# A hybrid decoder trunk: the last pair of output tiles of the first MLP as two plain tiles, and the mLSTM's sums of squares and gates three to five steps earlier

## The chip, the cores and the metric

The kernel runs on one core of one Trainium2 chip. The metric is the device time of one execution in microseconds (us), as the median of several runs. Engines are named as in the profile: PE is TensorE's matmul, PEld its weight load, DVE is VectorE, ACT is ScalarE, POOL is GpSimd, SP is SyncE, which issues most transfers. Times inside an execution are microseconds from the start of the profiled span.

## The reference

Two layers on 512 tokens of 1024 features. Layer 0 is a differential attention followed by an MLP; layer 1 is an mLSTM mixer followed by an MLP. Each part is normed on its way in and added back.

```python
for layer in range(DEPTH):                 # 2
    mix = diff_attention(rmsnorm(h, ...)) if layer == 0 else mlstm_mixer(rmsnorm(h, ...))
    h = h + mix
    h = h + sqrelu_mlp(rmsnorm(h, mlp_norm[layer]), mlp_w1[layer], mlp_w2[layer])
return rmsnorm(h, final_norm)

def sqrelu_mlp(h, w1, w2):                 # 1024 -> 4096 -> 1024
    return jnp.square(jax.nn.relu(h @ w1)) @ w2

def mlstm_mixer(h, w_in, b_i, b_f, conv_w, conv_b, head_norm_w, w_out):
    proj = h @ w_in                        # q and k, v, output gate, 2 x 4 gates
    ...
    i_pre = gates[..., :ML_HEADS] + b_i
    log_f = jax.nn.log_sigmoid(gates[..., ML_HEADS:] + b_f)
    ht = mlstm_chunkwise(q, k, v, i_pre, log_f)
```

## The kernel before

**Layout.** The residual `h` stays on the chip, transposed, as eight tiles `h[0]` to `h[7]` of 128 features by 512 tokens; `h2[i]` is the pair `h[2i]`, `h[2i+1]`. Products are made from split operands: a value is a high part in fp32r (made on ACT, line 254 at the bottom of `split` and `operand`) and a low part (the rest, made on DVE, line 528 or 513), and each product is three matmuls: high by high, low by high, high by low. Weights come in units of 512 KB: a DMA from SP into a `raw` tile, then a split into `whi` and `wlo`. There are three `raw`, `whi` and `wlo` tiles in a ring and one more of each (`rawx`, `whix`, `wlox`) inside an MLP.

**Steps.** PE's order is the order of the program. `tick()` counts steps: one step is three matmuls of 512 columns, or six of 264 in the mLSTM's first product. `after(n, f)` runs `f` n steps later, which puts f's matmuls at that place of PE's order. The other engines' instructions are put in order by the framework's scheduler, each engine in order from then on.

**The MLP.** `hidden` makes one hidden tile: ReLU, scaling, square, and sums and differences of blocks of 256 tokens in `chains`, seven blocks of which are split into a slot `uh`, `ul` (line 885). `down(q, i)` adds quarter q of the hidden tiles into the pair of output tiles i. It computes the 2 by 2 block product with seven block products in place of eight (28 steps: 7 products by 4 hidden pairs, by 3 matmuls of 256 columns, lines 922 to 924). For it the two weight units are split in four pieces: `first`, `half`, and two pieces of sums of weights (`sums1` and `sums2`, lines 365 to 370, results in `wsums`). Its results are joined on DVE in `work` (lines 937 to 940) and added to the pair at once (line 945); then each of the two tiles becomes the next part's operand: `x_xh` on ACT, its square on ACT, `x_xl` on DVE (line 513), and the square is added to `acc` on POOL (line 524). The last call is `down(3, 3)`, which makes `h[6]` and `h[7]`. In the second MLP that last pair is made in another way, by `finish`, with the blocks that `spare` keeps (line 887); this is there before and after.

**The mLSTM's start.** `vpair_mm(x, 264)` multiplies the first 256 value columns and the 8 gate columns: for each of the eight operand tiles k in turn, 12 matmuls (lines 432 to 434) into four banks. Then eight `ntile_mm` make the tiles of q and k (lines 400 to 402, 24 matmuls of 512 columns each), one of which goes through `evict_qk` when it is done: a product with the scale `rs` (line 1026), the convolution's three multiply-adds (line 1030), a sigmoid, a split.

- `token_scale` (T_MRS = 22 steps after the start): splits `acc`, sums it over features with two matmuls by `ones_d` (lines 535, 536), and makes the scale `rs` from it (lines 559, 552, 553, 561 on DVE; logarithm, exponential, table load, square on ACT).
- `gates` (T_GATES = 14 steps after the first product): `token_cols` turns `rs` with four transposes (line 569), DVE copies column `rscol` out of them, then come the gates and the eviction of the values (line 582). The third q and k tile takes the first of the value banks.
- `gate_rows` (T_GROWS = 30) transposes the gates (line 1067) and makes running sums on DVE (lines 1068 to 1082); `gate_cols` (T_GCOLS = 60) transposes the rows `ig` back (line 1087).
- `head(hd)` starts 15 steps after the last q and k tile: its `scores` are made of line 1106 (gates), exponentials on ACT, line 1117 and on.

## Time and profile before

| | us |
|---|---|
| median of 3 runs | 1186.81 (1186.56 to 1188.86) |
| the profiled execution | 1188.99 |
| its span in the profile | 1187.3 |
| PE busy | 1144.2 (96% of the span) |
| DVE busy | 915.3 (77%) |
| ACT busy | 608.5 (51%) |
| POOL busy | 184.6 (16%) |
| PE's share of the chain that ended last | 77% |
| DVE's share of it | 14% |

The profile is of one execution. The lines of the page that show busy shares cut the span into 40 slices of 29.7 us, in tenths; PEclk is the clock that was granted to TensorE, in tenths of 2.4 GHz. Matmuls are pipelined, so the distance between the starts of two matmuls, not the duration of one, is what PE needs for it. A number in brackets at the end of a row is the time that the engine sat idle before that instruction, with what released it.

### The profile page before, as it was taken

Reading aid. Unit: us, or ns where it says so; the run is one execution under the profiler, and the core shown is the slowest. Engines: PE = TensorE matmul, PEld = TensorE weight load, DVE = VectorE, ACT = ScalarE, POOL = GpSimd, SP = SyncE. Lnnn points to the kernel's source line nnn. Section 1 sums busy time; section 2 is a strip of 40 time slices with the busy share of each in tenths; the row PEclk is TensorE's granted clock in tenths of the full one; section 3 lists DMA queues with packets and bytes.
Section 4 is the critical chain, followed back from the end, with each engine's and each line's share of the span. In section 5 each row is a group of like instructions: output and inputs, shape, how many; then the busy total and the mean of one; then the engine's idle time right before and its main releaser. Section 6 shows DMA issues by size and latency. Waiting matters only on the chain.

```text
span 1187.3 us, 17224 instructions
## 1 busy us (share of the span) xinstructions
PE 1144.2 (96%) x6730; PEld 1006.3 (85%) x6730; DVE 915.3 (77%) x1384; ACT 608.5 (51%) x917; POOL 184.6 (16%) x178
## 2 busy tenths in 40 slices
PE   7799999999999999999988899999999999999996
PEld 5688888888998998998977778887889889889895
DVE  7679888577976967966979957667598688687786
ACT  5477777564534434534545457574454354353453
POOL 5432332040000000000221212224000000000001
PEclk9899999999999999999999999999999999999998
DMA  6622222243164273371231221223425524625412
GB/s 204 187 66 79 81 71 79 65 130 118 54 177 133 70 188 108 90 192 57 73 113 39 89 71 52 74 71 91 135 77 137 148 90 126 172 70 145 145 36 71
DMA packets 36593, 123.92 MB, mean 104 GB/s; under 512 B 4351, under 2 KB 6418, under 8 KB 36512
## 3 DMA queue, kind: packets, MB, share of 16 engines
q1 hardware_dynamic: 30288, 103.38, 27.6%
q0 software_dynamic: 5104, 17.87, 7.7%
q10 hardware_dynamic: 1120, 1.57, 0.4%
q8 instruction: 53, 0.87, 0.3%
q14 instruction: 28, 0.23, 0.1%
HBM read 108.11 MB, written 4.74 MB: 95 GB/s over the span
## 4 chain that ended last, share of the span: by engine, by line
PE 77%; DVE 14%; ACT 4%; issue 2%; DMA 2%; POOL 0%; DVEq 0%; SPq 0%; ACTq 0%; POOLq 0%
PE bank L401 15%; PE bank L402 15%; PE bank L400 15%; PE bank L923 8%; PE bank L924 8%; PE bank L922 8%; DVE wlo L528 2%; DVE tmp_tmp L1030 1%; PE bank L434 1%; PE bank L433 1%; PE bank L432 1%; DMA raw<-wgt 1%; DVE x_xl L513 1%; ACT whi L254 1%; PE bank L730 1%
## 5 line engine op out<-in xcount | busy, mean ns | idle before, releaser
L400 PE MATMUL bank<-x_xh,whi 128*128 128x512 f32 x640 | 253.5, 396 | 4.8 <-DVE vl_v L582 2.5
L402 PE MATMUL bank<-x_xh,wlo 128*128 128x512 f32 x640 | 255.0, 398 | 1.0 <-DVE wlo L528 1.0
L401 PE MATMUL bank<-x_xl,whi 128*128 128x512 f32 x640 | 254.4, 398 | 0.6 <-DVE x_xl L513 0.6
L254 ACT ACTIVATE whi<-raw 128x1024 fp32r<-128x1024 f32 (+2 forms) x128 | 133.4, 1043 | 124.5 <-PE bank L923 47.8
L528 DVE TENSOR_TENSOR wlo<-raw,whi 128x1024 fp32r<-128x1024 f32 (+2 forms) x128 | 160.6, 1255 | 34.3 <-ACT whi L254 33.7
L923 PE MATMUL bank<-ul,whi 128*128 128x256 f32 x560 | 157.8, 282 | 0.1
L922 PE MATMUL bank<-uh,whi 128*128 128x256 f32 x560 | 157.9, 282 | 0.0
L924 PE MATMUL bank<-uh,wlo 128*128 128x256 f32 x560 | 157.8, 282 | 0.0
L400 PEld LDWEIGHTS bank<-x_xh,whi 128*128 128x128 f32 x640 | 122.5, 191 | 32.9 <-DVE vl_v L582 3.0
L402 PEld LDWEIGHTS bank<-x_xh,wlo 128*128 128x128 f32 x640 | 120.9, 189 | 28.7 <-DVE wlo L528 1.9
L401 PEld LDWEIGHTS bank<-x_xl,whi 128*128 128x128 f32 x640 | 121.1, 189 | 27.9 <-DVE x_xl L513 1.3
L923 PEld LDWEIGHTS bank<-ul,whi 128*128 128x128 f32 x560 | 105.7, 189 | 0.5 <-DVE ul L528 0.3
L922 PEld LDWEIGHTS bank<-uh,whi 128*128 128x128 f32 x560 | 106.0, 189 | 0.1
L924 PEld LDWEIGHTS bank<-uh,wlo 128*128 128x128 f32 x560 | 105.8, 189 | 0.0
L943 POOL DMA_DIRECT2D h<-work x24 | 20.8, 866 | 510.9 <-DVE work L940 391.8
L254 ACT ACTIVATE uh<-chains 128x1792 fp32r<-128x1792 f32 (+1 forms) x35 | 55.6, 1588 | 57.7 <-DVE chains L883 57.6
L528 DVE TENSOR_TENSOR ul<-chains,uh 128x1792 fp32r<-128x1792 f32 (+1 forms) x35 | 66.0, 1886 | 23.6 <-ACT uh L254 23.4
L876 DVE SCALAR_TENSOR_TENSOR tmp_tmp<-bank,rs_rs 128x512 f32<-128x512 f32 x64 | 44.0, 688 | 46.1 <-PE bank L402 45.9
L524 POOL TENSOR_TENSOR acc_acc<-acc_acc,tmp_tmp 128x512 f32<-128x512 f32 x31 | 51.7, 1668 | 168.0 <-ACT tmp_tmp L254 167.0
L254 ACT ACTIVATE whi<-wsums 128x1024 fp32r<-128x1024 f32 x47 | 49.8, 1059 | 51.9 <-PE bank L923 30.3
L432 PE MATMUL bank<-whi,x_xh 128*128 128x256 f32 (+1 forms) x256 | 73.3, 286 | 1.8 <-ACT x_xh L254 1.8
L434 PE MATMUL bank<-whi,x_xl 128*128 128x256 f32 (+1 forms) x256 | 73.0, 285 | 0.8 <-DVE x_xl L513 0.7
(304 smaller groups left out, 2660.8 us busy)
## 6 DMA issues: line engine op xcount, KB each, us to landing
raw<-wgt SPq DMA_DIRECT2D x156, 512.0 KB, 3.7
rawx<-wgt SPq DMA_DIRECT2D x32, 512.0 KB, 3.8
h<-work POOLq DMA_DIRECT2D x24, 512.0 KB, 5.9
skew<-frd POOLq DMA_DIRECT2D x8, 320.0 KB, 7.6
bias_bias<-skew POOLq DMA_DIRECT2D x8, 256.0 KB, 3.0
outT<-h SPq DMA_DIRECT2D x6, 256.0 KB, 2.5
raw<-wgt SPq DMA_DIRECT2D x2, 528.0 KB, 3.7
h<-xT ACTq DMA_DIRECT2D x4, 256.0 KB, 5.7
```

What stands on the lines that cost most here:

```text
L254: ins = nc.scalar.activation(out, x, func, **kw)
L400: mm(ps, whi, x[0], start=first, stop=False)
L401: mm(ps, whi, x[1], start=False, stop=False)
L402: mm(ps, wlo, x[0], start=False, stop=last)
L432: mm(ps, xh, hi[:, c], start=k == 0, stop=False)
L434: mm(ps, xl, hi[:, c], start=False, stop=k == KT - 1)
L524: (eng or pool).tensor_tensor(acc, acc, s, op=ALU.add)
L528: (eng or vec).tensor_tensor(lo, src, asf(hi), op=ALU.subtract)
L876: vec.scalar_tensor_tensor(m, p, 0.0, rs, op0=ALU.max, op1=ALU.mult)
L922: mm(out[name], hi[:, n], uh[:, t], start=first, stop=False, skip_group_check=late)
L923: mm(out[name], hi[:, n], ul[:, t], start=False, stop=False, skip_group_check=late)
L924: mm(out[name], lo[:, n], uh[:, t], start=False, stop=k == 3, skip_group_check=late)
```

## The change

The seven-product form is left for the last pair of the first MLP, `(q, i) = (3, 3)`. Its two weight units are now split whole, like those of other products, without sums of weights. The hidden blocks that the seven products did not need (block 7) are now kept in the first MLP too (`if q == 3`), in `spare`: the second half of a `sh` tile or a slot that is free by then. `plain(3)` makes tile 6 and then tile 7: for each, four products over whole 512 tokens and four in two halves of 256, three matmuls each, 36 matmuls in 8 steps. After each tile, DVE adds its bank to `h[n]`, and the operand is made. And four numbers move the mLSTM's early work: T_MRS 22 to 17, T_GATES 14 to 10, T_GROWS 30 to 26, T_GCOLS 60 to 57. The local function `operands` is moved out, unchanged.

```diff
-T_GATES, T_GROWS, T_GCOLS, T_MRS = 14, 30, 60, 22
+T_GATES, T_GROWS, T_GCOLS, T_MRS = 10, 26, 57, 17
...
-                pair(m2, q, i, "plain" if last and (q, i) == (3, 3) else "pair")
+                pair(m2, q, i, "plain" if (q, i) == (3, 3) else "pair")
...
-                if finish is not None and q == 3:
+                if q == 3:
                     split(F[:, 7 * B :], *spare(i))
...
+            def plain(i):
+
+                for n in (2 * i, 2 * i + 1):
+                    hi, lo = unit()
+                    ps = bank()
+                    for k in (4, 5, 6, 7, 0, 1, 2, 3):
+                        w = slice(k * P, (k + 1) * P)
+                        if k >= 4:
+                            parts = [(slice(0, T), [z[:, : 2 * B] for z in slots[(8 + k) % 5]])]
+                        else:
+                            parts = [(slice(t * B, (t + 1) * B), operands(k, t)) for t in range(2)]
+                        for c, (a, b) in parts:
+                            end = k == 3 and c.stop == T
+                            mm(ps[:, c], hi[:, w], a, start=k == 4, stop=False, skip_group_check=True)
+                            mm(ps[:, c], hi[:, w], b, start=False, stop=False, skip_group_check=True)
+                            mm(ps[:, c], lo[:, w], a, start=False, stop=end, skip_group_check=True)
+                        tick()
+                    vec.tensor_tensor(h[n], h[n], ps, op=ALU.add)
+                    nxt.append(operand(n, g0, nacc))
...
+                elif (q, i) == (3, 3):
+                    plain(i)
```

DVE's order at the end of the last pair. `h_97` is the pair of tiles 4 and 5, `h_98` that of 6 and 7; `x_xl_240`, `_262`, `_280` and `_315` are the low operands of tiles 4 to 7; `wlo` rows are low parts of weights of the mLSTM. Before:

```order
L945 TENSOR_TENSOR h_97<-h_97,work 128x1024
L937 TENSOR_TENSOR work<-bank_84,work 128x2x256
L528 TENSOR_TENSOR wlo_93<-raw_87,whi_90 128x1024
L513 SCALAR_TENSOR_TENSOR x_xl_240<-h_97,colt,x_xh_239 128x512
L513 SCALAR_TENSOR_TENSOR x_xl_262<-h_97,colt,x_xh_261 128x512
L938 TENSOR_TENSOR work<-bank_83,work 128x512
L939 TENSOR_TENSOR work<-bank_82,work 128x512
L940 TENSOR_TENSOR work<-bank_83,work 128x256
L945 TENSOR_TENSOR h_98<-h_98,work 128x1024
L992 CAST sel<-tmp_tmp_233 128x512
```

After, at the same place:

```order
L945 TENSOR_TENSOR h_97<-h_97,work 128x1024
L981 TENSOR_TENSOR h_98<-h_98,bank_78 128x512
L528 TENSOR_TENSOR wlo_92<-raw_87,whi_89 128x1024
L513 SCALAR_TENSOR_TENSOR x_xl_240<-h_97,colt,x_xh_239 128x512
L513 SCALAR_TENSOR_TENSOR x_xl_262<-h_97,colt,x_xh_261 128x512
L513 SCALAR_TENSOR_TENSOR x_xl_280<-h_98,colt,x_xh_279 128x512
L981 TENSOR_TENSOR h_98<-h_98,bank_84 128x512
L1014 CAST sel<-tmp_tmp_233 128x512
L1018 TENSOR_SCALAR hw<-colt 128x8
L474 TENSOR_SCALAR gs<-ones_f 128x256 x3
L513 SCALAR_TENSOR_TENSOR x_xl_315<-h_98,colt,x_xh_314 128x512
```

Tile 6 is added and split ahead of tile 7's addition, and the four joins in `work` are gone. (Lines from 954 on stand 22 further down in the changed kernel.)

ACT and DVE around the scale `rs`. `chains` rows are the logarithm, the exponential and the square on ACT; `whi` and `wlo` rows are splits of weight units that stand among them. DVE before:

```order
L528 TENSOR_TENSOR sl_sl_333<-acc_acc_128,sh_sh_332 128x512
L528 TENSOR_TENSOR wlo_92<-raw_86,whi_89 128x1024
L559 TENSOR_SCALAR chains<-bank_82 128x512
L528 TENSOR_TENSOR wlo_93<-raw_87,whi_90 128x1024
L552 TENSOR_TENSOR chains<-chains 128x512
L553 SCALAR_TENSOR_TENSOR chains<-chains 128x512
L561 TENSOR_SCALAR rs_rs_183<-chains 128x512
L1026 TENSOR_TENSOR conv_5080<-bank_78,rs_rs_183 128x512
```

After:

```order
L528 TENSOR_TENSOR sl_sl_333<-acc_acc_128,sh_zeros 128x512
L528 TENSOR_TENSOR wlo_93<-raw_88,whi_90 128x1024
L528 TENSOR_TENSOR wlo_94<-raw_86,whi_91 128x1024
L559 TENSOR_SCALAR chains<-bank_78 128x512
L552 TENSOR_TENSOR chains<-chains 128x512
L553 SCALAR_TENSOR_TENSOR chains<-chains 128x512
L528 TENSOR_TENSOR wlo_92<-raw_87,whi_89 128x1024
L561 TENSOR_SCALAR rs_rs_183<-chains 128x512
L1048 TENSOR_TENSOR conv_5061<-bank_79,rs_rs_183 128x512
```

The split that stood between lines 559 and 552 now stands between 553 and 561; on ACT its high part stands behind the square in place of ahead of the exponential.

## Rows read from the trace of the kernel before

**Rows 1.** The page, busy tenths in 40 slices of 29.7 us, PE and DVE.

```profile
PE   7799999999999999999988899999999999999996
...
DVE  7679888577976967966979957667598688687786
```

**Rows 2.** Busy time by stretch, from the last pair of the first MLP to the first head's scores: stretch, its length, busy us and instructions of PE, PEld, DVE, ACT and POOL, granted clock, DMA share, GB/s.

```profile
584.20:595.70 11.50, 10.25 (x86) 10.05 (x85) 11.50 (x14) 5.51 (x8) 3.83 (x2) 1.00 0.22 66
595.70:612.10 16.40, 13.82 (x98) 13.10 (x97) 16.16 (x23) 7.50 (x11) 7.03 (x5) 0.90 0.33 100
612.10:628.40 16.30, 12.54 (x57) 9.65 (x55) 10.07 (x23) 8.69 (x13) 0.00 (x0) 1.00 0.33 98
628.40:635.60 7.20, 7.20 (x24) 5.75 (x25) 6.78 (x13) 4.57 (x8) 1.28 (x1) 0.76 0.18 58
635.60:667.90 32.30, 29.72 (x133) 23.45 (x132) 30.05 (x43) 15.13 (x23) 7.04 (x4) 1.00 0.20 58
667.90:686.20 18.30, 15.46 (x114) 14.21 (x112) 15.93 (x21) 9.91 (x16) 4.73 (x5) 1.00 0.28 83
```

**Rows 3.** PE in order of time, from the first matmul of the last pair to the first of the first q and k tile: start, duration, instruction.

```profile
584.21 0.28 PE L922 MATMUL bank<-uh,whi 128*128 128x256 f32 x1
...
588.62 0.28 PE L923 MATMUL bank<-ul,whix 128*128 128x256 f32 x1
590.15 0.39 PE L924 MATMUL bank<-uh,wlox 128*128 128x256 f32 x1 [1.25 <-DVE wlox L528]
...
595.73 0.29 PE L432 MATMUL bank<-whi,x_xh 128*128 128x264 f32 x1
...
604.34 0.28 PE L434 MATMUL bank<-whi,x_xl 128*128 128x264 f32 x1
606.43 0.39 PE L432 MATMUL bank<-whi,x_xh 128*128 128x264 f32 x1 [1.81 <-ACT x_xh L254]
...
607.67 0.39 PE L434 MATMUL bank<-whi,x_xl 128*128 128x264 f32 x1 [0.74 <-DVE x_xl L513]
...
612.14 0.46 PE L400 MATMUL bank<-x_xh,whi 128*128 128x512 f32 x1
```

**Rows 4.** PE later: the second and third q and k tile, and the last waits of the stretch.

```profile
622.19 0.40 PE L402 MATMUL bank<-x_xh,wlo 128*128 128x512 f32 x1
623.80 0.66 PE L569 MATMUL bank<-ident,rs_rs 128*128 128x128 f32 x4 [1.21 <-DVE rs_rs L561]
...
625.46 0.40 PE L402 MATMUL bank<-x_xh,wlo 128*128 128x512 f32 x1
628.40 0.50 PE L400 MATMUL bank<-x_xh,whi 128*128 128x512 f32 x1 [2.54 <-DVE vl_v L582]
...
664.87 0.22 PE L1087 MATMUL bank<-ident,ig 4*128 4x4 f32 x1 [1.55 <-DVE ig L1077]
...
686.20 0.44 PE L1106 MATMUL bank<-gs,sel 128*128 128x384 f32 x1 [2.34 <-ACT e_e L254]
```

**Rows 5.** DVE's low operands, alone and beside an addition on POOL, and POOL's rows at those times.

```profile
584.21 0.73 DVE L513 SCALAR_TENSOR_TENSOR x_xl<-h,colt,x_xh 128x512 fp32r<-128x512 f32 x1
...
585.47 1.78 DVE L513 SCALAR_TENSOR_TENSOR x_xl<-h,colt,x_xh 128x512 fp32r<-128x512 f32 x1
...
598.70 4.01 DVE L513 SCALAR_TENSOR_TENSOR x_xl<-h,colt,x_xh 128x512 fp32r<-128x512 f32 x2
...
584.50 3.91 POOL L524 TENSOR_TENSOR acc_acc<-acc_acc,tmp_tmp 128x512 f32<-128x512 f32 x2 [7.50 <-ACT tmp_tmp L254]
...
600.24 0.58 POOL L991 DMA_DIRECT2D tmp_tmp<-consts  x1 [0.30 <-POOL acc_acc L524]
```

**Rows 6.** DVE and ACT from the sums of squares to the first evicted value.

```profile
617.07 0.69 DVE L559 TENSOR_SCALAR chains<-bank 128x512 f32<-128x512 f32 x1 [2.32 <-PE bank L536]
...
621.87 0.69 DVE L552 TENSOR_TENSOR chains<-chains 128x512 f32<-128x512 f32 x1 [1.24 <-ACT chains L254]
...
623.32 0.43 DVE L561 TENSOR_SCALAR rs_rs<-chains 128x512 f32<-128x512 f32 x1
...
627.87 0.47 DVE L582 SCALAR_TENSOR_TENSOR vl_v<-bank,rscol_rscol,vh_v 128x256 fp32r<-128x256 f32 x1
...
618.33 1.04 ACT L254 ACTIVATE whi<-raw 128x1024 fp32r<-128x1024 f32 x1
619.27 0.62 ACT L254 ACTIVATE chains<-chains 128x512 f32<-128x512 f32 x1
619.91 1.28 ACT L245 ACT_TABLE_LOAD   x1
```

**Rows 7.** DVE's two longer waits of the stretch after that, and the issues of POOL's queue (line of the page: queue, count, KB, median us from issue to landing).

```profile
636.68 1.23 DVE L528 TENSOR_TENSOR wlo<-raw,whi 128x1024 fp32r<-128x1024 f32 x1 [1.23 <-ACT whi L254]
...
639.99 1.09 DVE L1030 SCALAR_TENSOR_TENSOR tmp_tmp<-conv,colt,tmp_tmp 128x512 f32<-128x512 f32 x1 [0.88 <-ACT tmp_tmp L254]
...
skew<-frd POOLq DMA_DIRECT2D x8, 320.0 KB, 7.6
...
tmp_tmp<-consts POOLq DMA_DIRECT2D x1, 256.0 KB, 3.8
```

**Rows 8.** The second MLP, which splits block 7 already: one such split on DVE, and busy times of the stretch around it (columns as in rows 2).

```profile
1119.01 0.43 DVE L528 TENSOR_TENSOR ul<-chains,uh 128x256 fp32r<-128x256 f32 x1
...
1060.00:1140.00 80.00, 79.90 (x537) 73.68 (x536) 61.30 (x80) 34.64 (x40) 3.44 (x4) 1.00 0.46 126
```

More of the change, by code (lines that the diff above doesn't have):

```diff
@@ L952, in down, with operands @@
                         square_in(n, finish.acc, vec if i == 2 else pool)
+            def operands(k, t):
+                s, j = k % 4, k // 4
+                hi, lo = slots[(12 + s) % 5]
+                block = (2, 7)[t] if j == 0 else t
+                if block == 7:
+                    return spare(s)
+                w = slice(block * B, (block + 1) * B)
+                return hi[:, w], lo[:, w]
+            def plain(i):
[16 more added lines that the diff above has]
+                    nxt.append(operand(n, g0, nacc))
             after(T_MLP, lambda: token_scale(acc, rs))
@@ L961, in mlp @@
                 elif finish is not None and (q, i) == (3, 3):
-                    def operands(k, t):
-                        s, j = k % 4, k // 4
-                        hi, lo = slots[(12 + s) % 5]
-                        block = (2, 7)[t] if j == 0 else t
-                        if block == 7:
-                            return spare(s)
-                        w = slice(block * B, (block + 1) * B)
-                        return hi[:, w], lo[:, w]
                     finish(operands)
+                elif (q, i) == (3, 3):
+                    plain(i)
                 else:
```

## The prediction

> **What bounds the kernel now.** I read the busy tenths first, then one stretch, then PE's waits in it. PE is busy in nine tenths or more of nearly every slice; only at the ends and in three slices from 594 us to 683 us does it fall to eight, and in that neighbourhood DVE stands at eight or nine [rows 1]. So the kernel is PE's, but this stretch, from the last pair of the first MLP to the first scores of the mLSTM, is shared. By stretch [rows 2]: DVE is busy 11.50 of 11.50 us during the last pair and 16.16 of 16.40 during the mLSTM's first product, so it enters that product in arrears; then it idles (10.07 of 16.30) while it waits for the sums of squares; then it is full again (30.05 of 32.30). PE's waits are what this costs [rows 3, 4]: 1.53 us between two starts for a split of weight sums; 2.09 and 1.02 us for the operands of tile 6; 1.61 us for `rs`; 2.94 us for a value bank; 1.55 us for `ig`; 2.34 us for an exponential. Twice the granted clock falls behind such a wait: to a mean of 0.90 and of 0.76, that is, for part of these stretches to the lower of its levels, 1.2 of 2.4 GHz; behind the wait for `rs` alone it stays at 1.00 [rows 2].
>
> Matmul prices are distances of starts. At 256 columns: 37 from 584.21 to 588.62, 0.119 us. At 264: 71 from 595.73 to 604.34, 0.121 us. At 512: 43 from 612.14 to 622.19 (24 of the first tile, the two sums, 17 more), 0.234 us [rows 3, 4].
>
> **The last pair on PE.** Before: 84 matmuls of 256 columns and the wait, 584.21 to 595.73, 11.52 us [rows 3]. After: 24 of 512 and 48 of 256, 24 × 0.234 + 48 × 0.119 = 11.33 us. Plain work costs 1.3 us more than 84 × 0.119 = 10.0, the wait for sums of weights pays that back: **-0.2 us**, product start at 595.5. Here a page speaks: the Trainium skill, TensorE: Matmul & The Clock Gate, section "Back-to-back issue gap", gives about 131 ns a matmul for a sustained stream of 512 columns. By it the pair would end 24 × 0.103 = 2.5 us sooner and the sum would be -10.5 us; the trace has 0.234 and decides, so this gets no chance of its own.
>
> **The mLSTM's first product.** Before 595.73 to 612.14, 16.41 us; 96 × 0.121 = 11.6 without a wait or a fall of the clock: **-4.8 us**, end at 607.2 [rows 3]. This holds if tiles 6 and 7 come in time; they are asked for 72 and 84 matmuls in, at 604.3 and 605.7. I follow DVE by its new order, with the durations of the same kinds of rows; the times are estimates. Gone from it are four joins, five sums and differences of weights, a half and a second split of sums; the pair's one addition becomes two halves, and one plain split comes in: about seven microseconds less between 580 and 606. So the pair (4, 5) is added by 592.8, tile 6 (finished by PE at 589.9) by 593.4, and then, behind one weight split, come three low operands. Alone one takes 0.73 us, beside an addition on POOL 1.78 to 2.0 [rows 5]; at the dear price they end at 600.0. Tile 7's addition ends at 600.6, its high part on ACT at 601.4, its low part, behind `sel` and three fills, at 603.5. That is over two microseconds early. The squares of tile 7 pass POOL by 603.5 and the split of `acc` ends near 605.5.
>
> **Sums of squares at step 17.** They now stand one step into the first q and k tile, at 607.2 + 0.7 = 607.9, and their operands are ready at 605.5: no wait. Behind them DVE has the second weight split first (its bank of weights is read until 607.2, ACT 1.04, DVE 1.23: 609.5). Then line 559 (0.69), logarithm and exponential (0.63 each), table load 1.28, square 0.63, lines 552 and 553 (0.7 each), a weight split that used to stand elsewhere (1.15), line 561 (0.43): `rs` at 616.4, against 623.75 before [rows 6]. That is 7.35 us earlier. Bounds: 5.5, if the two splits and POOL slow DVE throughout, to 8.5, if both splits slip in without a wait.
>
> **Gates four steps earlier.** PE reaches the transposes of `rs` after 26 + 6 matmuls of 512 columns, at 614.7, and waits until 616.45: 1.8 us against 1.4, **+0.4 us**. What queues behind it is PE alone, all of it. The rest of the second tile is 18 × 0.234 + 0.4: it ends at 621.1. From the copy of `rscol` to the end of the first evicted value took 3.84 us (624.50 to 628.34) [rows 6]; from 617.2 that gives 621.05. So the third tile no longer finds its bank taken: the wait of 2.94 less a normal 0.23 goes, **-2.6 us** [rows 4], and with it the fall of the clock, 24 matmuls in 7.20 us against 5.6 [rows 2], **-1.6 us**. PE's ledger to the end of the third tile: -0.2 - 4.8 + 0.4 - 2.6 - 1.6 = -8.8 us.
>
> **What is late next.** From `rs` on, DVE is full to 683 us, so its ledger counts: 7.35 us earlier at `rs`, and of its two waits of 1.23 and 0.88 us [rows 7] about 1.0 comes back in another form (the third tile's convolution waits for ACT), so 8.5. `gate_rows` four steps earlier adds no instruction, it lets the copies of the gates fill one of those waits. `gate_cols` three steps earlier lets PE stand: PE, 8.8 + 3 × 0.7 us earlier and without the wait that it had, would arrive near 651, and DVE has the last `ig` 8.5 us ahead of 664.8, at 656.3: a wait of some five microseconds in place of 1.55 [rows 4], with seven more steps (4.9 us) to do behind it, in place of four. The second value product then starts near 661.3 against 667.9, 6.6 us earlier. The second scores, reached at 683.7, waited until 686.20 for an exponential [rows 4], which hangs on DVE's last convolution: 8.5 earlier that is 677.7, and PE is there at 677.1. One weight split of DVE waits for the eighth tile on PE and may take up to 1.0 us of this; I take half. **Sum at the first scores: -8.0 us.** From there to the end nothing is changed, and PE waits little.
>
> **Edits costed at nothing.** Four splits of 256 columns on ACT and DVE (0.42 and 0.43 each) during the fourth quarter. The second MLP has them already: there PE is busy 79.90 of 80 us [rows 8]. Bounds 0 to 0.2 us; without that cover 4 × 0.4. The weight transfers are the same in number and size. SP issues them when DVE lets a `raw` tile go, which is now earlier.
>
> **Against its own time.** The profiled execution took 1188.99 us, 1.7 more than its span of 1187.3. The median is 1186.81; I take the difference from it: 1186.8 - 8.0 = **1178.8 us**.
>
> **Rivals.**
> - *The bank still waits.* DVE's arrears are longer than I count, `rs` moves with the product's end only, and the third tile waits as before. Then the first three terms remain: -0.2 - 4.8 + 0.4 = -4.6, 1182.2 us. For it: DVE is full in both stretches [rows 2] and what I give its rows beside POOL is an estimate from three of them [rows 5]. Against it: it is idle for six microseconds between 612 and 628. 0.16.
> - *The clock falls at `ig`.* Twice a wait above two microseconds on PE was followed by a lower granted clock [rows 2 to 4]; the new wait of five is longer than either. Price: 1.6 us, as from 628.4 to 635.6; PE then comes to the scores at 678.7 and is the late one. 1180.4 us. A page supports this: the Trainium skill, same page, section "HAM oscillation", says that gaps in PE's activity bring the clock back to its lower level, and that each costs anew; by this rule the longer wait brings the fall back, and the trace agrees with the rule at two places. 0.12.
> - *`sel` holds DVE: not faster, or slower.* DVE's copy of `sel` waits for a transfer that POOL's queue issues between its additions (600.24 before [rows 5]; near 596.4 after), and now stands ahead of tile 7's low operand and the split of `acc`. It lands in 3.8 us by its row, 7.6 by the slowest of that queue [rows 7]; there are 2.8 us to spare beyond 3.8. Past that each microsecond is one lost on PE, with 1.6 for the clock. From a landing of about 13 us nothing is gained, at 16 it is 1188.4 us. Against it: no row that long. 0.06 for no change, 0.06 for slower.
>
> That the change does not do what it says is excluded by the order of instructions.
>
> **How the numbers follow.** Forecast 0.60, the rivals 0.16, 0.12 and 0.12. The range of the forecast alone: `rs` between 5.5 and 8.5 earlier, and the clock after the scores, which falls now and may not then, about 1 us more: 1176.0 to 1181. To leave out no more than 0.2 it must reach over the two milder rivals, with a microsecond for what differs between runs: 1176.0 to 1183.4. A measurement of this kernel can tell about 0.2% (2.4 us) from no change. Faster by more than that: 0.60 + 0.16 + 0.12 = 0.88; within it 0.06; slower 0.06.
>
> **What would show it.** Right: no wait inside the last pair and in the 96 matmuls of the first product, which take about 11.6 us; `rs` seven microseconds earlier; the third q and k tile starting at most 0.5 us behind the second; a longer wait at the transposes of `ig`, and the first scores near 678 us of the span. Wrong: a wait for an `x_xl` of tile 7 in the first product, a wait at line 535 for the split of `acc`, DVE idle ahead of `sel`, or a second tile of the second value product late by as much as was gained.

## The result and the profile after

The changed kernel takes **1181.48 us** (median of 7 runs, 1179.17 to 1182.15), the kernel before 1186.81 in the same comparison (7 runs, 1183.51 to 1188.86). The ratio of the two is 0.9943, with a 95% interval from 0.9928 to 0.9958: 5.0 to 8.5 us faster, 6.8 in the middle. In a second comparison (6 and 11 runs) the medians are 1179.46 and 1186.44, the ratio 0.9944 (0.9923 to 0.9965). The profiled execution took 1181.82 us with a span of 1180.0, 7.3 less than before.

One thing has to be taken out before the two traces are laid side by side. In fourteen profiled executions of these kernels the mLSTM's first product begins anywhere from 592.92 to 597.92 us after the span's start. Most of that is settled early: in the first 100 us the profile of before has 436 PE rows and a mean granted clock of 0.97, that of after 430 and 0.95; the trace in which the product begins first has 456 rows there, the one in which it begins last 415. The last pair begins at 584.93 us in after and at 584.21 in before, so 0.7 us was lost ahead of it, where the change only adds the four splits of block 7. I therefore count from the start of the last pair, or of the first product.

The page after, busy tenths of PE and DVE (to [rows 1]):

```profile
PE   8899999999999999999999899999999999999996
...
DVE  7679888586977866967979867666597688687786
```

Of the three slices near the mLSTM's start in which PE stood at eight, one is left. Stretches of the trace of after (columns as in [rows 2]): last pair, first product, first two q and k tiles, third tile, on to the last transpose of `ig`, the rest of the eighth tile, second value product, second scores.

```profile
584.90:596.20 11.30, 11.30 (x74) 10.28 (x73) 11.27 (x13) 7.43 (x12) 5.29 (x5) 1.00 0.49 157
596.20:607.90 11.70, 11.70 (x98) 11.70 (x97) 8.53 (x16) 2.83 (x4) 5.10 (x3) 1.00 0.16 51
607.90:622.05 14.15, 12.35 (x56) 9.67 (x55) 9.24 (x21) 7.95 (x12) 0.00 (x0) 1.00 0.37 110
622.05:627.60 5.55, 5.55 (x25) 4.55 (x25) 4.38 (x11) 5.44 (x9) 1.30 (x1) 1.00 0.00 1
627.60:657.00 29.40, 24.44 (x112) 19.43 (x110) 29.15 (x43) 14.22 (x21) 6.20 (x3) 0.97 0.24 72
657.00:664.50 7.50, 7.50 (x23) 5.98 (x23) 7.17 (x10) 1.54 (x5) 2.44 (x1) 0.65 0.38 113
664.50:679.60 15.10, 15.10 (x114) 14.15 (x112) 11.33 (x14) 9.30 (x15) 4.75 (x4) 1.00 0.16 49
679.60:690.00 10.40, 9.13 (x43) 7.48 (x43) 7.95 (x13) 5.37 (x11) 2.08 (x3) 1.00 0.34 102
```

PE is full in the first two stretches, and the clock is at its upper level up to the transposes of `ig`. During the wait ahead of the last of them it falls (0.97 in the stretch that ends there), and over the 7.50 us behind it the mean is 0.65. Behind the second scores, where it fell before, it now stays at 1.00. The ten microseconds behind them in before:

```profile
686.20:696.20 10.00, 9.66 (x37) 7.84 (x38) 6.79 (x11) 4.96 (x10) 0.95 (x2) 0.83 0.29 97
```

PE's rows in after, in order of time (to [rows 3, 4]):

```profile
584.93 0.39 PE L977 MATMUL bank<-uh,whi 128*128 128x512 f32 x1
...
596.21 0.28 PE L432 MATMUL bank<-whi,x_xh 128*128 128x264 f32 x1
...
607.95 0.39 PE L400 MATMUL bank<-x_xh,whi 128*128 128x512 f32 x1
...
617.36 0.66 PE L569 MATMUL bank<-ident,rs_rs 128*128 128x128 f32 x4 [1.80 <-DVE rs_rs L561]
...
622.05 0.41 PE L400 MATMUL bank<-x_xh,whi 128*128 128x512 f32 x1
...
653.07 0.22 PE L1109 MATMUL bank<-ident,ig 4*128 4x4 f32 x1 [1.25 <-DVE ig L1099]
657.00 0.26 PE L1109 MATMUL bank<-ident,ig 4*128 4x4 f32 x1 [3.71 <-DVE ig L1099]
...
664.50 0.28 PE L432 MATMUL bank<-whi,x_xh 128*128 128x256 f32 x1
...
679.30 0.40 PE L402 MATMUL bank<-x_xh,wlo 128*128 128x512 f32 x1
679.58 0.45 PE L1128 MATMUL bank<-gs,sel 128*128 128x384 f32 x1
681.29 0.44 PE L1139 MATMUL bank<-qk_qkh,qk_qkh 128*128 128x384 f32 x1 [1.27 <-DVE e_e L1142]
...
725.91 0.50 PE L1139 MATMUL bank<-qk_qkh,qk_qkh 128*128 128x512 f32 x1 [1.23 <-ACT rs_rs L254]
```

The last pair takes 596.21 - 584.93 = 11.28 us (11.52 before), the first product 11.74 (16.41 before), neither with a wait. The third q and k tile starts at 622.05 without one. The new wait for `ig` is 1.25 + 3.71 = 4.96 us. The last row is a landmark for all that follows: a matmul of a later score that waits 1.2 us for ACT in every kernel here. In before it is this one:

```profile
733.18 0.50 PE L1117 MATMUL bank<-qk_qkh,qk_qkh 128*128 128x512 f32 x1 [1.24 <-ACT rs_rs L254]
```

From the start of the last pair the landmark comes after 140.98 us in after and 148.97 in before: **8.0 us earlier**.

DVE from tile 6's operand to `rs` in after (to [rows 5, 6]):

```profile
594.01 5.70 DVE L513 SCALAR_TENSOR_TENSOR x_xl<-h,colt,x_xh 128x512 fp32r<-128x512 f32 x3
599.64 0.68 DVE L981 TENSOR_TENSOR h<-h,bank 128x512 f32<-128x512 f32 x1
600.24 0.42 DVE L1014 CAST sel<-tmp_tmp 128x512 fp32r<-128x512 f32 x1
...
601.25 0.74 DVE L513 SCALAR_TENSOR_TENSOR x_xl<-h,colt,x_xh 128x512 fp32r<-128x512 f32 x1
...
615.75 1.22 DVE L528 TENSOR_TENSOR wlo<-raw,whi 128x1024 fp32r<-128x1024 f32 x1
616.89 0.42 DVE L561 TENSOR_SCALAR rs_rs<-chains 128x512 f32<-128x512 f32 x1
```

There is no idle time ahead of `sel`; the three low operands beside POOL cost 1.90 us each; tile 7's low operand is there at 601.99, over four microseconds before PE asks for it. `rs` is there at 617.31, that is 32.38 us after the start of the pair, against 39.54 before.

One more place is needed below. Ahead of the second scores DVE has a weight split (`wlo`) whose high part (`whi`, on ACT) needs the tile that the eighth q and k tile still reads. In after, ACT, DVE, and then the exponential that the scores take:

```profile
664.47 1.06 ACT L254 ACTIVATE whi<-raw 128x1024 fp32r<-128x1024 f32 x1 [0.93 <-PE bank L401]
665.56 1.23 DVE L528 TENSOR_TENSOR wlo<-raw,whi 128x1024 fp32r<-128x1024 f32 x1 [1.30 <-ACT whi L254]
...
678.96 0.56 ACT L254 ACTIVATE e_e<-bank,rc 128x384 f32<-128x384 f32 x1
```

DVE waits 1.30 us for it. The exponential ends at 679.53 (678.96 and 0.56, rounded), 0.05 us ahead of the scores, and PE, one matmul of 0.23 us behind 679.30, is free at the same moment.

### The profile page after: what moved, and what is told of

Same layout as the page of the kernel before. It is cut to its first block, busy times and chain, and to the rows that moved or that the text cites. A ratio compares the mean times of both kernels' runs of the same rounds, so it can differ in the third digit from the quotient of the medians.

```text
span 1180.0 us, 17195 instructions
## 1 busy us (share of the span) xinstructions
PE 1145.0 (97%) x6718; PEld 1008.3 (85%) x6718; DVE 907.8 (77%) x1379; ACT 608.7 (52%) x918; POOL 187.5 (16%) x178
## 4 chain that ended last, share of the span: by engine, by line
PE 62%; issue 17%; DVE 12%; ACT 5%; DMA 3%; POOL 1%; DVEq 0%; SPq 0%; POOLq 0%; ACTq 0%
PE bank L401 12%; PE bank L402 12%; PE bank L400 11%; PE bank L923 5%; PE bank L924 5%; PE bank L922 5%; DVE wlo L528 2%; DMA raw<-wgt 1%; PE bank L433 1%; PE bank L432 1%; PE bank L434 1%; DMA h<-work 1%; DVE tmp_tmp L1052 1%; PE bank L730 1%; ACT chains L254 1%
## 5 line engine op out<-in xcount | busy, mean ns | idle before, releaser
L923 PE MATMUL bank<-ul,whi 128*128 128x256 f32 x544 | 153.3, 282 | 0.1
L922 PE MATMUL bank<-uh,whi 128*128 128x256 f32 x544 | 153.3, 282 | 0.0
L924 PE MATMUL bank<-uh,wlo 128*128 128x256 f32 x544 | 153.2, 282 | 0.0
L923 PEld LDWEIGHTS bank<-ul,whi 128*128 128x128 f32 x544 | 102.7, 189 | 0.6 <-DVE ul L528 0.3
L922 PEld LDWEIGHTS bank<-uh,whi 128*128 128x128 f32 x544 | 103.0, 189 | 0.1
L924 PEld LDWEIGHTS bank<-uh,wlo 128*128 128x128 f32 x544 | 102.8, 189 | 0.0
L433 PE MATMUL bank<-wlo,x_xh 128*128 128x256 f32 (+1 forms) x256 | 72.1, 282 | 0.0
```

Of the source, the lines that this page charges most:

```text
L433: mm(ps, xh, lo[:, c], start=False, stop=False)
L922: mm(out[name], hi[:, n], uh[:, t], start=first, stop=False, skip_group_check=late)
L923: mm(out[name], hi[:, n], ul[:, t], start=False, stop=False, skip_group_check=late)
L924: mm(out[name], lo[:, n], uh[:, t], start=False, stop=k == 3, skip_group_check=late)
```

## Experiments

Each is a small edit of one of the two kernels, or of another edited one, as the diffs say; `after_again` is after once more. For all of them, three times from their traces, in us from the first matmul of the first product: the end of `rs` on DVE, the first matmul of the second scores (the one of 384 columns by `sel`), and the landmark. For after these are 617.31 - 596.21 = 21.10, 679.58 - 596.21 = 83.37 and 725.91 - 596.21 = 129.70. The ratio is to the kernel before in the same comparison, with its 95% interval.

| kernel | `rs` | scores | landmark | ratio |
|---|---|---|---|---|
| before | 28.02 | 90.47 | 137.45 | 1 |
| after | 21.10 | 83.37 | 129.70 | 0.9943 (0.9928 to 0.9958) |
| after_again | 21.10 | 83.32 | 129.68 | 0.9944 (0.9923 to 0.9965) |
| plain_only | 23.25 | 85.66 | 132.78 | 0.9956 (0.9938 to 0.9974) |
| numbers_only | 25.83 | 88.24 | 134.62 | 0.9974 (0.9959 to 0.9990) |
| splits_only | 26.92 | 87.83 | 134.82 | 0.9998 (0.9980 to 1.0015) |
| gcols64 | 21.10 | 82.53 | 129.36 | 0.9931 (0.9906 to 0.9957) |
| mrs22 | 23.25 | 85.69 | 131.16 | 0.9954 (0.9939 to 0.9968) |
| gates14 | 21.09 | 87.99 | 132.70 | 0.9963 (0.9948 to 0.9977) |
| dve_more | 21.10 | 86.12 | 134.22 | 0.9980 (0.9964 to 0.9995) |
| early_sums | 16.94 | 80.17 | 128.18 | 0.9927 (0.9907 to 0.9947) |
| early_act | 16.93 | 79.46 | 127.34 | 0.9937 (0.9917 to 0.9956) |
| early_fill | 16.94 | 80.18 | 126.65 | 0.9927 (0.9909 to 0.9945) |
| early_both | 16.93 | 79.49 | 125.83 | 0.9921 (0.9903 to 0.9938) |

The intervals are 3 to 6 us wide, so differences of 1 or 2 us between two of these kernels are read from the traces, and are only as good as one execution of each. The trace of after, taken twice, gave the same three times within 0.05 us.

### The two halves apart, and the added splits

`plain_only` is the changed kernel with the four numbers of before; `numbers_only` the kernel before with the four new numbers; `splits_only` the kernel before with the splits of block 7 alone.

```diff
 plain_only, from after
-T_GATES, T_GROWS, T_GCOLS, T_MRS = 10, 26, 57, 17
+T_GATES, T_GROWS, T_GCOLS, T_MRS = 14, 30, 60, 22
 numbers_only, from before
-T_GATES, T_GROWS, T_GCOLS, T_MRS = 14, 30, 60, 22
+T_GATES, T_GROWS, T_GCOLS, T_MRS = 10, 26, 57, 17
 splits_only, from before
-                if finish is not None and q == 3:
+                if q == 3:
```

> The changed kernel with the four numbers of before (14, 30, 60, 22): the plain last pair alone. Theory (the two parts add up, each through its own waits): the last pair and the first product lose their waits as in the changed kernel (pair about 11.3 us, 96 matmuls about 11.7 us), which is about -4.6 us at the sums of squares; rs comes about 4.5 us earlier, the third q and k tile still waits about 2.5 us for its value bank and the clock still falls behind it, and ig waits 1 to 2 us. Time against before -4 to -5 us, 1182 to 1183. Rival (the numbers give nothing, the plain pair is all of it): as fast as the changed kernel, -6.5 to -7.5 us. Second rival (the pair gives nothing without the numbers, since DVE sets the scores): within 1.5 us of before.

> The kernel before with the four numbers of the changed one (10, 26, 57, 17): the seven-product pair is kept. Theory: the first product keeps its waits (2.1 and 1.0 us) and its fall of the clock, 16.4 us; the sums of squares stand 5 steps earlier, rs comes about 3.4 us earlier, near 620.4; PE waits under 1 us for it; the third tile's bank wait of 2.5 us and the clock fall behind it go; ig waits 3 to 5 us. Time against before -2 to -3.5 us. Rival (the earlier sums only move a wait, since the split of acc is not ready): within 1 us of before, with a wait at the sums of 1 us or more.

> The kernel before with the four added splits of block 7 and nothing else (their results are not read). Theory: they cost 0 to 0.2 us, PE stays busy through the fourth quarter. Rival: they push DVE back ahead of the last pair, whose weight sums and tile 6 then come later: 0.4 to 1.7 us slower.

PE in `plain_only`, at the transposes of `rs` and the third q and k tile:

```profile
618.21 0.33 PE L569 MATMUL bank<-ident,rs_rs 128*128 128x128 f32 x1 [1.17 <-DVE rs_rs L561]
...
622.81 0.50 PE L400 MATMUL bank<-x_xh,whi 128*128 128x512 f32 x1 [2.56 <-DVE vl_v L582]
```

PE in `numbers_only`, at the sums of squares and the last transpose of `ig`:

```profile
610.62 0.40 PE L535 MATMUL bank<-sh_sh,ones_d 128*128 128x512 f32 x1
...
658.98 0.26 PE L1087 MATMUL bank<-ident,ig 4*128 4x4 f32 x1 [3.71 <-DVE ig L1077]
```

Both behave as the first theory says, with one miss: in `numbers_only` I had `rs` 3.4 us earlier and under 1 us of wait for it, and found 2.2 and 1.80. The plain pair alone brings the landmark 137.45 - 132.78 = 4.7 us nearer to the first product and keeps the wait for the bank (2.56 us); 0.2 us more comes from the pair itself. The numbers alone bring 2.8 us: the sums find their operand ready, and the wait for `ig` appears in full (3.71 us at its last transpose). 4.7 + 2.8 = 7.5 against 7.75 for both. The ratios, 0.9956 and 0.9974, go the same way. By them the rivals "nothing without the numbers" and "the sums only move a wait" fall; "all of it is the pair" falls by the traces alone, since the intervals of `plain_only` and after overlap.

The added splits cost nothing that can be measured (0.9998). The interval alone does not exclude the rival's 0.4 to 1.7 us, but its mechanism is not there: PE waits 1.27 us for the weight sums where before had 1.25, and 1.82 for tile 6 where before had 1.81. Their trace even has the landmark 2.6 us earlier, and this shows how chance of the clock enters a single trace: the same waits for tile 6 (1.82 and 0.74 us) were followed by a fall of the clock in before and not here, so that the first product took 15.38 us in place of 16.41, at 1.00 throughout:

```profile
596.83:612.21 15.38, 12.44 (x98) 11.80 (x97) 15.14 (x22) 7.07 (x11) 7.04 (x5) 1.00 0.35 108
```

### Where the scores hang: DVE or PE

`gcols64` moves `gate_cols` behind the last q and k tile, where PE need not wait for `ig`. `dve_more` adds work to DVE on top of that.

```diff
 gcols64, from after
-T_GATES, T_GROWS, T_GCOLS, T_MRS = 10, 26, 57, 17
+T_GATES, T_GROWS, T_GCOLS, T_MRS = 10, 26, 64, 17
 dve_more, from gcols64, in evict_qk
                 vec.tensor_tensor(xs[:, 4:], ps, rs, op=ALU.mult)
+                if tile_i in (1, 2, 5, 6):
+                    vec.tensor_tensor(xs[:, 4:], ps, rs, op=ALU.mult)
```

> The changed kernel with gate_cols at step 64 in place of 57, behind the last q and k tile. Theory A (DVE's convolutions set the second head's scores, as the prediction has it): PE's wait of 5.0 us for ig falls below 1 us and the clock stays up behind it, the second value product starts 6 to 7 us earlier, but the scores then wait for DVE: the second scores come only 0.5 to 2 us earlier than in the changed kernel, since only DVE's waits for weight splits (1.3 and 1.9 us) can shrink. Time -0.5 to -2 us against the changed kernel. Theory B (what PE lost at ig, 5.0 us and about 2.4 us of clock, is lost for good): -5 us or more against the changed kernel. Theory C (rc, which gate_cols gives, comes too late for the first scores): slower than the changed kernel by 1 us or more, with a wait on rc.

> The changed kernel with gate_cols at step 64 and, in the eviction of q and k, the product with rs done twice for four of the eight tiles (the same values once more): 4 times 0.69 = 2.8 us of added work on DVE between rs and the second scores. Theory (DVE's ledger from rs on sets those scores): they come 2 to 2.8 us later than in the kernel with gate_cols at 64 alone, and the time is 2 to 2.8 us longer. Rival (PE, or ACT's splits of weights, sets them): under 1 us.

PE in `gcols64`: the start of the second value product and the second scores. Under them the busy times of the ten microseconds behind (columns as above).

```profile
658.61 0.38 PE L432 MATMUL bank<-whi,x_xh 128*128 128x256 f32 x1
...
679.00 0.58 PE L1128 MATMUL bank<-gs,sel 128*128 128x384 f32 x1 [2.35 <-ACT e_e L254]
```

```profile
678.80:688.80 10.00, 9.59 (x37) 7.78 (x38) 6.85 (x11) 5.18 (x11) 1.18 (x3) 0.83 0.29 102
```

Theory A holds for the scores; at the landmark the gain is just under its 0.5 to 2 us. The wait for `ig` is gone, and counted from the first product the second value product starts 68.29 - 62.14 = 6.15 us earlier than in after; yet the scores come only 0.84 us earlier, since there PE now waits 2.35 us for the exponential. Behind that wait the clock falls (0.83 over ten microseconds), and at the landmark 0.34 us is left. So what PE loses at `ig` in after is nearly all slack. The 0.84 us pass through DVE: with the eighth tile done earlier, the weight split for which DVE waits 1.30 us in after comes here without a wait,

```profile
664.84 1.22 DVE L528 TENSOR_TENSOR wlo<-raw,whi 128x1024 fp32r<-128x1024 f32 x1
```

and DVE's last convolution, and the exponential behind it, are earlier by the same 0.8 us.

PE in `dve_more`, at the same scores:

```profile
679.04 0.69 PE L1130 MATMUL bank<-gs,sel 128*128 128x384 f32 x1 [4.48 <-ACT e_e L254]
```

The 2.8 us of added work put the scores 86.12 - 82.53 = 3.6 us back and the landmark 4.9: more than the theory's 2 to 2.8, in its direction, far from the rival's "under 1". The wait of 4.48 us is followed by a deeper fall of the clock, which would account for the step from 3.6 to 4.9. That four rows of 0.69 us became 3.6 is mostly DVE's order. Busy times from the end of `rs` to DVE's first row of the second scores, in `gcols64` and in `dve_more`:

```profile
617.57:676.03 58.46, 56.01 (x289) 47.23 (x290) 55.43 (x89) 30.18 (x46) 12.77 (x7) 0.97 0.24 72
614.02:675.78 61.76, 56.92 (x290) 46.99 (x290) 58.67 (x93) 31.54 (x48) 11.62 (x7) 0.97 0.23 69
```

DVE does 58.67 - 55.43 = 3.24 us more there; 2.67 are the four rows, and a weight split of 1.2 us that stood behind this place now stands ahead of it.

### The numbers one by one

```diff
 mrs22, from after
-T_GATES, T_GROWS, T_GCOLS, T_MRS = 10, 26, 57, 17
+T_GATES, T_GROWS, T_GCOLS, T_MRS = 10, 26, 57, 22
 gates14, from after
-T_GATES, T_GROWS, T_GCOLS, T_MRS = 10, 26, 57, 17
+T_GATES, T_GROWS, T_GCOLS, T_MRS = 14, 30, 57, 17
```

> The changed kernel with the sums of squares back at step 22 (T_MRS alone). Theory (the time of rs sets everything up to the first scores, because all of DVE's work of the stretch hangs on it): rs comes 3 to 3.5 us later than in the changed kernel, PE waits 4.5 to 5.5 us for it at the transposes in place of 1.8, the scores come about 3 us later; +2.5 to +3.5 us against the changed kernel. Rival (DVE and PE catch up before the scores, since PE stands idle for 5 us at ig anyway): within 1 us of the changed kernel.

> The changed kernel with the gates and their rows back at steps 14 and 30 (sums at 17 and columns at 57 stay). Theory (the wait for rs and the wait for a value bank are one wait in two places: moving the gates by four steps turns one into the other): no wait for rs at the transposes, a wait of 2 to 2.6 us for the bank at the third q and k tile; rscol 0.5 to 0.8 us later; the scores, which hang on DVE, 0 to 1 us later: 0 to +1.5 us against the changed kernel (the upper end if the clock falls behind that wait). Rival (as the prediction has it, the gates' steps pay 2.6 us of bank wait and 1.6 us of clock): +2.5 to +4 us.

PE in `mrs22`, at the transposes of `rs`:

```profile
619.85 0.33 PE L569 MATMUL bank<-ident,rs_rs 128*128 128x128 f32 x1 [3.97 <-DVE rs_rs L561]
```

PE in `gates14`, at the third q and k tile and the last transpose of `ig`:

```profile
622.08 0.77 PE L400 MATMUL bank<-x_xh,whi 128*128 128x512 f32 x1 [3.27 <-DVE ab L1073]
...
659.82 0.26 PE L1109 MATMUL bank<-ident,ig 4*128 4x4 f32 x1 [5.45 <-DVE ig L1099]
```

With the sums at step 22 PE issues them 3.5 us later from the first product's start, but `rs` is only 2.15 us later, the scores 2.32, and the landmark 1.46: part of the delay is made up on the way. At the scores PE is the late one here: the exponential is there 0.95 us before them. My theory had the direction and about twice the size; by the trace the rival's "within 1 us" is missed as well, by the ratios it can't be told.

`gates14` refutes my theory for it. The wait for `rs` does turn into a wait at the third tile, but the tile's wait is 3.27 us, and the last transpose of `ig` comes 64.97 - 60.79 = 4.2 us later than in after. PE, not DVE, then brings the scores, 4.6 us later: the exponential is there 2.5 us before them. 3.0 us are lost at the landmark, inside the rival's 2.5 to 4. The prediction's own terms for the gates make 3.8 us to the end of the third tile (2.6 + 1.6, less the 0.4 at `rs`); there `gates14` is 34.31 - 31.41 = 2.9 us behind after, from the first product. The 5.45 us at `ig` come later, and how much of the 3.0 is theirs is not shown.

### Earlier sums, and filling PE's waits

In after the split of `acc` is ready at 605.3 us (it starts at 604.65 and takes 0.69), over three microseconds ahead of the sums at 608.64. `early_sums` uses this. `early_act` takes two copies off DVE; `early_fill` lets PE multiply by a tile of zeros where it would stand still; `early_both` has the two edits together.

```diff
 early_sums, from after
-T_GATES, T_GROWS, T_GCOLS, T_MRS = 10, 26, 57, 17
+T_GATES, T_GROWS, T_GCOLS, T_MRS = 8, 24, 62, 14
 early_act, from early_sums, in gate_rows
-                    vec.tensor_copy(dst, ps[0:MH])
+                    act(dst, ps[0:MH], AF.Copy)
 early_fill, from early_sums, in scores (filler(n): n matmuls none x x_xh into the open output-gate tile;
   its definition and that of the zero tile none are left out here)
+                    if (hd, j) == (0, 1):
+                        filler(10)
                     pg = bank("sc")
...
+                    if (hd, j) == (0, 1):
+                        filler(5)
                     ps = bank("sc")
```

> The changed kernel with the sums of squares at step 14 (inside the first product), the gates at 8, their rows at 24 and their columns at 62. The split of acc was ready at 605.3 us of the changed kernel's span, and step 14 of the product falls at 606.5. Theory (rs sets the stretch): rs 3 to 3.7 us earlier than in the changed kernel, no wait over 1 us for ig, scores 3 us earlier; -2 to -3.5 us against the changed kernel. Rival (with rs so early, PE is the bound: nothing stands still any more, and the last gain is PE's alone): -1 to -2 us, PE without a wait between 608 us and the scores. Second rival (the sums now wait on PE for the split of acc, or the weight split ahead of the logarithm holds it back): no gain.

> The kernel early_sums with the two copies of the gates' rows out of their banks (0.67 us each on DVE) on ACT. Theory (DVE's ledger sets the second scores): these come 1.0 to 1.4 us earlier than in early_sums, counted from the first product; time -0.5 to -1.4 us against early_sums, as the clock behind the scores' wait allows. Rival (ACT, with its table load of 1.28 us and its splits, is the late one): no gain, or up to 1 us lost.

> The kernel early_sums with 15 added matmuls of zero weights (they add zero to the open output-gate tile) where PE stands still: ten ahead of the second scores' first matmul (2.39 us of wait in early_sums), five ahead of the next (1.21 us). Theory (the fall of the clock behind those two waits is caused by the standing still, and is what eats the gain between the scores and the end): the clock stays at 1.00 in the 10 us behind them (0.78 and 0.88 in early_sums), the scores come no later, and the rest comes 1.2 to 1.7 us earlier: -1.2 to -1.7 us against early_sums. Rival (the clock falls all the same, or its fall hides behind waits for DVE): within 0.5 us. Second rival (the added matmuls delay the scores): slower by up to 3.5 us.

> early_act and early_fill together: by the theories of both, -1.7 to -3 us against early_sums, 1176 to 1177.5; by their rivals within 1 us of early_sums.

> The changed kernel once more, unchanged, on the same chip as the three below, as their yardstick and as a second profiled execution. Theory (the clock's fall behind the wait for ig belongs to the kernel): a wait of 4.5 to 5.5 us for ig again, and behind it 21 matmuls of 512 columns in over 6.5 us in place of 4.9; 5.5 to 8 us faster than before. Rival (that fall was chance of one execution): under 5.5 us for the 21 matmuls.

PE in `early_sums` at the second scores, and the ten microseconds from there:

```profile
676.51 0.44 PE L1128 MATMUL bank<-gs,sel 128*128 128x384 f32 x1 [2.39 <-ACT e_e L254]
678.16 0.44 PE L1139 MATMUL bank<-qk_qkh,qk_qkh 128*128 128x384 f32 x1 [1.21 <-DVE e_e L1142]
```

```profile
676.30:686.30 10.00, 8.58 (x32) 6.91 (x33) 5.59 (x11) 4.61 (x9) 1.72 (x3) 0.83 0.26 86
```

The same two places in `early_fill`:

```profile
674.96 2.49 PE L431 MATMUL bank<-x_xh,none 128*128 128x512 f32 x10
677.47 0.44 PE L1139 MATMUL bank<-gs,sel 128*128 128x384 f32 x1
677.75 1.32 PE L431 MATMUL bank<-x_xh,none 128*128 128x512 f32 x5
```

```profile
677.30:687.30 10.00, 9.91 (x45) 7.88 (x45) 6.96 (x12) 5.26 (x11) 2.23 (x4) 1.00 0.26 84
```

`early_sums` makes `rs` 4.2 us earlier than after, more than expected, and the scores 3.2 us earlier; but only 1.5 us is left at the landmark, which is the first rival's figure and not its reason, for PE did wait (2.24 us for a bank near 651 us, then the 2.39 and 1.21 above). `early_fill` shows where the rest went. Its scores come at the same time (80.18 against 80.17), the clock behind them stays at its upper level, and the landmark is 1.53 us nearer, inside the 1.2 to 1.7 expected. That is what the theory says: the standing still brings the fall, and the fall costs time. `early_both` repeats it (no fall there), as `early_act` repeats the fall without the added matmuls. It stays short of proof: waits of this length went without a fall in `splits_only` and `gcols64` too, and the ratios of `early_sums` and `early_fill`, 0.9927 both, do not tell the two apart. `early_act` moves the scores by 0.71 us and the landmark by 0.84, below the 1.0 to 1.4 of the theory, above its rival.

By its trace `early_both` is 3.9 us ahead of after at the landmark (125.83 against 129.70). On one chip with after its median is 1177.53 us against 1179.46, and the ratios are 0.9921 and 0.9944; the intervals overlap, so that it beats before is shown, that it beats after is likely and not shown.

In `after_again` the wait for `ig` and the fall behind it are there again:

```profile
658.72 0.26 PE L1109 MATMUL bank<-ident,ig 4*128 4x4 f32 x1 [3.71 <-DVE ig L1099]
...
666.17 0.28 PE L432 MATMUL bank<-whi,x_xh 128*128 128x256 f32 x1
```

7.45 us for the same 21 matmuls of 512 columns that took 7.50 in the first trace, where 21 x 0.234 = 4.9 would do. That fall belongs to the kernel.

## Why the prediction came out as it did

**Right, by its own steps.** The last pair: -0.24 us (-0.2). The first product: -4.67 (-4.8), without a wait. `rs`: 7.16 us earlier from the pair's start (7.35). The wait at the transposes of `rs`: 1.80 (1.8). The third tile's bank wait and the fall of the clock behind it: gone; its end, at 627.62, is 8.7 us earlier counted from the pair (8.8). The wait for `ig`: 4.96 us ("some five"). The working behind that one had a gap: 664.87 less the 1.55 us of wait, 8.8 and 2.1 is 652.4, not "near 651". PE did come at 651.1 in the times of before, since one more wait went, which neither the sum nor [rows 4] names:

```profile
654.89 0.50 PE L402 MATMUL bank<-x_xh,wlo 128*128 128x512 f32 x1 [1.03 <-DVE wlo L528]
```

DVE was not idle ahead of `sel`, and the splits of block 7 cost nothing that can be seen. `plain_only` and `numbers_only` confirm the split between the two parts: I had -5.0 for the pair and the product, 4.9 was measured.

**The step that failed** is the choice between the forecast and the second rival. The forecast had PE leave the wait for `ig` at full clock, start the second value product 6.6 us earlier and reach the scores ahead of DVE, and gave the fall behind `ig` a chance of 0.12. The fall came, in both traces of after. The product starts 79.57 us after the pair's start against 83.69: 4.1 us earlier. The second scores start at 94.65 against 101.99, 7.3 us earlier and not 8.0. In the times of before PE is free for them at 678.8 us, where the forecast had 677.1 and the rival 678.7. But PE is not the late one, as the rival has it: the exponential ends at that same moment, so DVE's side was late too. Of the weight split that waits for the eighth tile the forecast took half of 1.0 us; it cost DVE 1.30, and `gcols64`, where PE neither waits at `ig` nor slows behind it, has no such wait and its scores 0.84 us earlier.

The rows to see the fall were there: the waits of 2.09 and 2.94 us between starts in [rows 3, 4] had a lower clock behind them in [rows 2], the 2.34 us ahead of the scores too (0.83, above), and the forecast made one longer than any of them. The price was too small as well: 7.50 - 4.91 = 2.6 us, in place of 1.6. And the rival's total did not follow from its own times: scores at 678.7 are 7.5 us ahead of 686.20, which gives 1179.3 us and not 1180.4. The Trainium skill, TensorE: Matmul & The Clock Gate, section "HAM oscillation", which I had put beside that rival, says that gaps in PE's work bring its clock down and that each return is paid for anew; the traces agree with it for all nine waits of 3.27 to 5.45 us (the 4.96 us for `ig` were followed by a mean of 0.65), and not for every shorter one (last section).

**Why the total still fits.** What the wait and the fall took was mostly slack: `gcols64`, without them, is 0.84 us better at the scores. And the fall behind the second scores, 0.83 in the ten microseconds from 686.20 us of before, did not come in after (1.00), where PE reached them without a wait; that the missing wait is the reason is likely and not shown. The prediction kept about 1 us for that in its range; from scores to landmark after is 0.65 us shorter (129.70 - 83.37 = 46.33 against 46.98), although it has 1.27 us of wait at the second matmul where before had 0.34. All told the trace has 7.34 + 0.65 = 8.0 us at the landmark. That this is the predicted sum is luck: the scores came 0.7 us short, and a gain of the same size behind them, which the forecast had only in its range, made up for it.

**The size.** Measured is 6.8 us by the ratio (5.0 to 8.5), against 8.0. The 1178.8 us lie 2.7 below the median of the first comparison and 0.7 below that of the second. The difference of 1.2 us between ratio and trace can't be settled: runs of one kernel spread over three to eight microseconds, and one trace shows one outcome of the clock.

**The other rivals.** The bank did not make PE wait, and `sel` held nothing back.

## What to carry to other kernels

A matmul engine that waits can pay twice, once for the wait and once for the clock behind it; price a new wait of several microseconds with its fall from the start, and ask of every wait that goes whether the next one takes its fall over. When one engine sets a later meeting point, moving another engine's work towards it only moves where that engine stands still: here the scores hung on DVE, and what helped, by the traces, was an earlier `rs`, less work on DVE, or work for PE while it waits. Numbers that place steps work together: with the gates at 10 the sums at 17 bring 1.46 us at the landmark (`mrs22` against after); with the gates at 14 the sums at 17 and the columns at 57 bring 0.08 (`plain_only` against `gates14`).

## What the runs showed of the hardware

- **Waits and the clock.** The nine longest waits of PE that the traces show between the last pair and the scores (3.27 to 5.45 us, in five kernels, after in both its traces) were followed by a granted clock below 1.00. Of the shorter ones, between 2.0 and 2.6 us, most were, and some were not: 2.40 us in `gcols64`, 2.55 in `splits_only` and 2.09 in `early_both` were not, 2.24 in `early_sums` was. Even 1.81 us for `rs` was in `gcols64`, where 1.80 in after was not. What decides between them no run here shows.
- **Work without use in a wait.** With fifteen matmuls of zero weights in waits of 2.39 and 1.21 us the clock behind them was 1.00, without them 0.83, and the stretch behind was 1.5 us shorter, by one trace each. In `early_both` the clock is 1.00 from the first product to the landmark.
- **The same kernel, the same fall.** In its two traces after has the same fall at the same place within 0.05 us, although the two began 1.7 us apart; but an edit that should not matter (`splits_only`) changed which of its waits the clock fell behind.
